# An encoder trunk on one core: first transfers in the order of need, the second chunk of x turned later, inverse square roots by three Newton steps

## The chip, the cores and the metric

The kernel runs on one core of one Trainium2 chip. The metric is device time of one launch in microseconds. TensorE is called PE, VectorE DVE, ScalarE ACT, GpSimd POOL; SP is the engine that only issues transfers. ACT and POOL issue transfers too, each in its own queue.

## The reference

Two layers over 512 tokens of 1024 features, all in float32. Each layer normalises x, projects it by one combined matrix, runs two attentions (a windowed one with 8 query and 2 key heads, and one over a two-dimensional neighbourhood with 8 heads), mixes them by sigmoid gates, and adds a SwiGLU block. The start of the first layer is what matters here:

```python
def rms_norm(x, g):
    xf = x.astype(jnp.float32)
    y = xf * lax.rsqrt(jnp.mean(xf * xf, axis=-1, keepdims=True) + EPS)
    return (y * g.astype(jnp.float32)).astype(x.dtype)
...
    for l in range(DEPTH):
        h = rms_norm(x, attn_norm_g[l])
        z = jnp.einsum('bsd,dc->bsc', h, w_in[l])
        qa, ka, va, qb, kb, vb, ga, gb = jnp.split(z, IN_SPLITS, axis=-1)
        qa = apply_rope(rms_norm(qa.reshape(b, s, A_HEADS, HEAD_DIM), q_norm_a[l]), cos, sin)
        ka = apply_rope(rms_norm(ka.reshape(b, s, A_KV_HEADS, HEAD_DIM), k_norm_a[l]), cos, sin)
```

Every normalisation is an inverse square root, of the whole row or of each head's 64 features.

## The kernel before, in words

Every float32 operand is split in a high part and a low part, and a product is three matmuls: high by high, high by low, low by high. Activations lie transposed, features on the partitions: x is eight chunks of 128 features by 512 tokens. The scaling by the row's inverse square root is applied after the products, so they need not wait for it.

**The start.** x comes in eight transfers of 256 KB on SP's queue (`x_load`, line 720), in pieces of 512 bytes. The weights of the first projection (queries, 512 columns) come as four slabs of 512 KB, two chunks each (`first_load`, line 536): the first on ACT's queue in two halves, the others on POOL's. PE warms up with seven products of a zero tile (`turn_over`, line 707). `token_matmul` (line 905) then takes the chunks: `begin(k)` is `start` (line 1209), which turns chunk k by four matmuls with an identity, has ACT make the high part of chunk k, a copy and its squares, and DVE the low part, the sum of squares and the weights' low part (`first_parts`, line 548; the weights' high part is a cast by ACT, by DVE for chunk 0). For a chunk, twelve products follow in three groups of four (one for each block of 128 tokens): high x by high weight, high x by low weight, low x by high weight. Behind a chunk's first group stands the turn of the chunk two further on:

```python
            begin(0)
            begin(1)
            tick(0.0)
```

so chunks 0 and 1 are turned ahead of the first product.

**Inverse square roots.** `rsqrt` (line 832) starts from an integer shift of the bits and refines by four Newton steps of three DVE instructions each. It is called twelve times: for each layer twice for the rows' norm (4 columns) and four times for the heads' (`head_scale`: 32 columns three times, 8 columns once).

**What sets the order.** The program is written by Python in one pass that keeps a clock for each engine. The main stream of products yields after each unit; attention heads, tables and norms are chains that are let in (`issue`, line 394) where the clocks say their operands are ready. Weight slabs are issued by the position of PE's stream (`tick`). The pass runs once dry, to learn when each buffer lives, then buffers are packed into two arenas, and the pass runs again and replays the choices. So a change of the first instructions or of a cost moves later choices too. Whether ACT or DVE scales a block of probabilities is such a choice. A transfer's completion is counted on one of eight semaphores of its kind in turn; a transfer that takes one again waits for the one that had it.

Of the kernel before, what the change touches and what calls it, by code (L numbers as in the profile page):

```python
# [12 lines left out]
F32 = mybir.dt.float32  # L13
# [3 lines left out]
ALU = mybir.AluOpType  # L17
AX = mybir.AxisListType

P = 128  # L20
# [5 lines left out]
KD = D // P  # L26
# [183 lines left out]
def trunk(ctx: ExitStack, tc: tile.TileContext, a: dict, out: bass.AP, lay: Layout):  # L210
    nc = tc.nc
    PS = bass.MemoryType.PSUM
    cp = ctx.enter_context(tc.tile_pool(name="cp", bufs=1))
# [7 lines left out]
    def nm(s):  # L221
        uid[0] += 1
        return f"{s}_{uid[0]}"
# [7 lines left out]
    def buf(shape, dtype=F32):  # L231

        n = int(np.prod(shape))
        x = lay.place(n, dtype)
        t = arenas[dtype][:, x : x + n]
        if len(shape) == 2:
            t = t.rearrange("p (a b) -> p a b", b=shape[1])
        elif len(shape) == 3:
            t = t.rearrange("p (a b c) -> p a b c", b=shape[1], c=shape[2])
        return t  # L240
# [7 lines left out]
    def mm_bank():  # L248
        return pm.tile([P, S], F32, tag="mm", name=nm("mm"))
# [4 lines left out]
    def small(w, dtype=F32):  # L254
        return sp.tile([P, w], dtype, tag=f"s{w}_{dtype}", name=nm("sm"), bufs=6)
# [81 lines left out]
    V = Engine(nc.vector, "dve")  # L337
    A = Engine(nc.scalar, "act")
    G = Engine(nc.gpsimd, "pool")
    Q = Engine(nc.sync, "dma")  # L340
    AQ = Engine(nc.scalar, "dma")
# [95 lines left out]
    def tick(dt):  # L437
        pos[0] += dt
        while due and due[0][0] <= pos[0]:
            due.pop(0)[2]()  # L440
# [79 lines left out]
    highs, lows, raws, used = {}, {}, {}, [0]  # L520
# [12 lines left out]

    FIRST = KD // 2

    def first_load(i):

        n1, n2, ((_, ap),) = plan[i]
        raws[i] = buf([n1, n2])
        ap = ap.rearrange("(k p) n -> p k n", p=P)  # L540
        if i:
            GQ.dma_start(raws[i], ap)
        else:
            for k in range(2):
                AQ.dma_start(raws[i][:, k], ap[:, k])
        highs[i], lows[i] = buf([n1, n2], F32R), buf([n1, n2], F32R)

    def first_parts(k):
# [25 lines left out]
    def w_take():  # L574

        i = used[0]
        used[0] += 1
        w_load(i)
        w_low(i)
        return [(highs[i][:, k], lows[i][:, k]) for k in range(plan[i][0])]  # L580
# [108 lines left out]
    def mm(ps, l_, r_, start, stop):  # L689
        T.matmul(ps, l_, r_, start=start, stop=stop, skip_group_check=True)  # L690
# [11 lines left out]
    ones = cp.tile([P, 2], F32, tag="ones", name="ones")  # L702
# [4 lines left out]
    def turn_over(n):  # L707

        ps = mm_bank()
        for _ in range(n):  # L710
            T.matmul(ps[:, :P], idle, idle, start=True, stop=True)
# [8 lines left out]
    def x_load(c):  # L720
        t = act().rearrange("p (b n) -> p b n", b=NB)
        Q.dma_start(t, xv[:, :, P * c : P * c + P])
        xin.append(t)
# [3 lines left out]
    Q.dma_start(ident, a["consts"][:, :P])  # L727
    rows_of = lambda n: a[n].rearrange("l (k p) -> (l k) p", p=P)
    AQ.dma_start(vec, rows_of("attn_norm_g"))
    first_load(0)  # L730
    AQ.dma_start(vec2[16:32], rows_of("ffn_norm_g"))
    for c in range(KD):
        x_load(c)
    first_load(1)
    posi = cp.tile([P, P], I32, tag="posi", name="posi")
    for h in range(2):
        GQ.dma_start(
# [3 lines left out]
    def gains_b(i, n):  # L741
        for h in range(2):
            GQ.dma_start(vec2[2 * i : 2 * i + 2, HD * h : HD * h + HD], a[n])

    gains_b(0, "q_norm_b")
    gains_b(1, "k_norm_b")
    first_load(2)
    first_load(3)
    gqa = cp.tile([P, 2, DEPTH, HD], F32, tag="gqa", name="gqa")
# [2 lines left out]
    snk = cp.tile([P, DEPTH, 8], F32, tag="snk", name="snk")  # L752
    GQ.dma_start(snk, a["sink_a"].rearrange("l h -> (l h)").unsqueeze(0).to_broadcast([P, DEPTH * 8]))
    GQ.dma_start(cst[:, P:], a["consts"][:, P:])
    warm = cp.tile([P, 2], F32, tag="warm", name="warm")
    A.copy(warm, ones)
    turn_over(7)
    ps = at_bank()
    T.transpose(ps[:, :16], vec, ident[:16, :16])
# [71 lines left out]

    def rsqrt(dst, src, w):

        ki, y, t = small(32, I32), small(32), small(32)
        V.tensor_scalar(ki[:, :w], src.bitcast(I32), 1, None, ALU.logical_shift_right)
        V.tensor_tensor(y[:, :w].bitcast(I32), magic[:, :w], ki[:, :w], ALU.subtract)
        for it in range(4):
            V.tensor_tensor(t[:, :w], y[:, :w], y[:, :w], ALU.mult)
            V.scalar_tensor_tensor(t[:, :w], t[:, :w], -0.5, src, ALU.mult, ALU.mult)
            V.scalar_tensor_tensor(dst if it == 3 else y[:, :w], t[:, :w], 1.5, y[:, :w], ALU.add, ALU.mult)  # L840

    class Norm:

# [17 lines left out]
        def chain(self):  # L861

            yield Need(keys=[f"acc{self.i}"])
            yield Need("pe", [self.acc], [at_slots])
            at_slots.take()
            ps = at_bank()
            for b in range(NB):
                T.matmul(ps[:, b : b + 1], self.acc[:, P * b : P * b + P], ones[:, 0:1], start=True, stop=True)
            ms = small(32)
            V.tensor_scalar(ms[:, :NB], ps[:, :NB], 1.0 / D, EPS, ALU.mult, ALU.add)  # L870
            at_slots.give(clock["dve"])
            self.rst = cp.tile([P, NB], F32, tag="rstd", name=nm("rstd"), bufs=2)
            rsqrt(self.rst, ms[:, :NB], NB)
            done.add(f"rst{self.i}")
            yield Need("pe", [self.rst], [at_slots])
            at_slots.take()
            ps = at_bank()
            for b in range(NB):
                T.transpose(ps[:, P * b : P * b + P], self.rst[:, b : b + 1].to_broadcast([P, P]), ident)
            self.rows = buf([S])  # L880
            V.tensor_copy(self.rows, ps)
            at_slots.give(clock["dve"])
            done.add(f"rows{self.i}")
# [21 lines left out]
    def token_matmul(nrm, evac, begin=None):  # L905

        ps = [mm_bank() for _ in range(NB)]
        if begin is not None:
            begin(0)
            begin(1)  # L910
            tick(0.0)
        for k0 in range(0, KD, 2):
            wk = w_take()
            order = [(b, k) for b in range(NB) for k in range(2)]
            if begin is not None:
                order.sort(key=lambda x: x[1])
                if k0 + 2 < KD:
                    for k in range(2):
                        kk = k0 + k
                        for part in range(3):  # L920
                            for b in range(NB):
                                x = (nrm.xl if part == 2 else nrm.xh)[kk][:, P * b : P * b + P]
                                mm(ps[b], x, wk[k][part == 1], kk == part == 0, False)
                            if not part and kk + 2 < KD:
                                begin(kk + 2)
                            tick(NB * UNIT / 3)
                            yield UNIT
                    continue
            for i, (b, k) in enumerate(order):
                t = slice(P * b, P * b + P)  # L930
                kk = k0 + k
                hi, lo = wk[k]
                mm(ps[b], nrm.xh[kk][:, t], hi, kk == 0, False)
                mm(ps[b], nrm.xh[kk][:, t], lo, False, False)
                mm(ps[b], nrm.xl[kk][:, t], hi, False, kk == KD - 1)
                tick(UNIT)
                if kk == KD - 1:
                    evac(b, ps[b])
                yield UNIT
# [5 lines left out]
    def head_scale(raw, nh, rst, res):  # L945

        ss = small(32)
        for b in range(NB):
            yield Need("act", [raw[b]])
            sq = act()  # L950
            A.activation(sq[:, : nh * HD], raw[b], AF.Square)
            yield Need("dve", [sq])
            V.tensor_reduce(ss[:, b * nh : b * nh + nh], per_head(sq[:, : nh * HD]), AX.X, ALU.add)
        yield Need()
        w = NB * nh
        rb = rst.unsqueeze(2).to_broadcast([P, NB, nh])
        v = lambda t: t[:, :w].rearrange("p (b h) -> p b h", h=nh)
        t = small(32)
        V.tensor_tensor(v(t), v(ss), rb, ALU.mult)
        V.tensor_tensor(v(t), v(t), rb, ALU.mult)  # L960
        V.tensor_scalar(t[:, :w], t[:, :w], 1.0 / HD, EPS, ALU.mult, ALU.add)
        f = sp.tile([P, 32], F32, tag="hf", name=nm("hf"), bufs=4)
        rsqrt(f[:, :w], t[:, :w], w)
        V.tensor_tensor(v(f), v(f), rb, ALU.mult)
        res.append(f)
# [263 lines left out]
    def layer(l):  # L1229
# [173 lines left out]
        spawn(chain_parts())  # L1403

        yield from token_matmul(nrm, copy_to(qraw), (lambda *x: start(nrm, *x)) if l == 0 else None)
        done.add(f"q{l}")

# [8 lines left out]
        for i, unit in enumerate(pair_matmul(KD, nrm.xh, nrm.xl, kv_evac)):  # L1416
            yield unit
            if i == KD:
                yield f"rows{nrm.i}"
        done.add(f"kv{l}")  # L1420
        yield from token_matmul(nrm, copy_to(qk[0]))
        done.add(f"qk{l}0")

# [370 lines left out]
```

## Time and profile before

| what | us |
|---|---|
| three timed runs | 1381.34 (median), 1382.67, 1380.99 |
| the profiled execution, its own time | 1382.42 |
| its span on the core | 1380.6 |
| PE busy | 1371.4 (99%) |
| weight loads of PE (beside its matmuls) | 1215.7 (88%) |
| DVE, ACT, POOL busy | 909.6, 708.8, 316.2 |

The span runs from the first to the last instruction on the core; the execution's own time has 1.8 us around it. Weight loads run beside matmuls and are counted apart. [...]

### The profile page before, as it was taken

To read this page: it belongs to the slowest core of one execution; us is meant where nothing else is said; L and a number is where in the kernel's file an instruction comes from. 1 tells how busy PE (TensorE), PEld (TensorE's weight loads), DVE (VectorE), ACT (ScalarE), POOL (GpSimd) and SP (SyncE) were. 2 spreads that over 40 slices of the span, in tenths; PEclk is the share of its full clock that TensorE was granted. 3 is DMA by queue.
4 is the path that set the end of the run, shared out by engine and by line. 5 is a ranking of instruction groups with operands and counts; after the bars stand their busy time and mean duration, and the time that the engine had idled before them with its cause. 6 is when DMAs were issued, how large, how long until landed. Compare 5 with 4: busy or idle time off the path is not lost.

```text
span 1380.6 us, 20976 instructions
## 1 busy us (share of the span) xinstructions
PE 1371.4 (99%) x8074; PEld 1215.7 (88%) x8074; DVE 909.6 (66%) x1700; ACT 708.8 (51%) x1174; POOL 316.2 (23%) x327
## 2 busy tenths in 40 slices
PE   8999999999999999999999999999999999999998
PEld 7888888888899999999888888888889999999997
DVE  5876878455966657575648668784568747575653
ACT  6477667534744333343545675684456434333441
POOL 4542222310311110111353422222012110111111
PEclk9999999999999999999999999999999999999999
DMA  8997888973766484734899978879439483655536
GB/s 215 180 176 136 165 154 155 180 190 104 151 152 153 111 195 91 183 93 92 170 192 191 167 136 156 165 138 233 120 93 214 104 214 93 153 121 124 132 67 153
DMA packets 192357, 207.48 MB, mean 150 GB/s; under 512 B 25584, under 2 KB 159136, under 8 KB 192256
## 3 DMA queue, kind: packets, MB, share of 16 engines
q0 software_dynamic: 132928, 141.54, 54.9%
q1 hardware_dynamic: 58832, 63.91, 16.1%
q8 instruction: 64, 1.05, 0.3%
q10 hardware_dynamic: 496, 0.67, 0.2%
q14 instruction: 37, 0.30, 0.1%
HBM read 193.51 MB, written 2.10 MB: 142 GB/s over the span
## 4 chain that ended last, share of the span: by engine, by line
PE 94%; DVE 2%; issue 1%; DMA 1%; POOL 1%; ACT 1%; SPq 0%; POOLq 0%; ACTq 0%; DVEq 0%
PE mm L310 72%; PE at L310 21%; DVE arena L310 1%; POOL arena L310 1%; DVE sm L310 1%; DMA arena<-in_w_in 1%; DMA arena<-in_x 1%; ACT arena L310 1%; ACT L310 0%; SPq L310 0%; DVE hf L310 0%; ACT trig L310 0%; ACT sm L310 0%; DVE den L310 0%; POOLq L310 0%
## 5 line engine op out<-in xcount | busy, mean ns | idle before, releaser
L310 PE MATMUL mm<-arena 128*128 128x512 f32 (+1 forms) x5568 | 1109.0, 355 | 0.2
L310 PEld LDWEIGHTS mm<-arena 128*128 128x128 f32 x5568 | 904.2, 190 | 131.4 <-issue 0.6
L310 ACT CAST arena<-arena 128x1024 fp32r<-128x1024 f32 (+2 forms) x277 | 234.6, 871 | 212.3 <-DVE arena L310 205.2
L310 DVE TENSOR_TENSOR arena<-arena,arena 128x1024 fp32r<-128x1024 f32 (+2 forms) x268 | 262.0, 993 | 48.3 <-ACT arena L310 44.3
L310 PE MATMUL at<-arena 128*128 128x256 f32 (+1 forms) x1964 | 285.0, 289 | 0.3 <-DVE negm L310 0.2
L310 ACT ACTIVATE arena<-arena 128x1024 fp32r<-128x1024 f32 (+3 forms) x252 | 207.0, 843 | 150.1 <-DMA arena<-in_w_down 63.9
L310 PEld LDWEIGHTS at<-arena 128*128 128x128 f32 x1964 | 261.7, 191 | 14.1 <-DVE negm L310 1.2
L310 DVE TENSOR_TENSOR arena<-arena,mm 128x512 f32<-128x512 f32 x144 | 98.7, 685 | 242.3 <-PE mm L310 240.7
L310 POOL DMA_DIRECT2D arena<-in_w_in x163 | 161.8, 1367 | 307.2 <-ACT arena L310 289.4
L310 POOL DMA_DIRECT2D arena<-in_w_down x96 | 99.2, 1230 | 508.9 <-ACT arena L310 310.6
L310 DVE TENSOR_TENSOR arena<-arena 128x1024 f32<-128x1024 f32 (+3 forms) x196 | 158.1, 823 | 2.3
L310 DVE TENSOR_TENSOR arena<-at,arena 128x512 fp32r<-128x512 f32 (+4 forms) x158 | 104.2, 660 | 31.6 <-ACT arena L310 22.6
L310 ACT CAST arena<-at 128x512 fp32r<-128x512 f32 (+2 forms) x116 | 64.3, 554 | 62.6 <-PE at L310 61.2
L310 ACT ACTIVATE arena<-arena,negm 128x256 f32<-128x256 f32 (+1 forms) x128 | 68.2, 533 | 18.7 <-DVE negm L310 16.9
L310 PE MATMUL at<-cst,arena 128*128 128x128 f32 x472 | 72.6, 276 | 4.0 <-DMA arena<-in_x 3.8
L310 PEld LDWEIGHTS at<-cst,arena 128*128 128x128 f32 x472 | 57.7, 141 | 13.4 <-DMA arena<-in_x 4.1
L310 DVE TENSOR_TENSOR arena<-mm,arena 128x512 f32<-128x512 f32 x72 | 49.1, 687 | 22.7 <-PE mm L310 22.3
L310 ACT COPY arena<-at 128x512 f32<-128x512 f32 (+1 forms) x72 | 41.3, 585 | 43.5 <-PE at L310 42.9
L310 DVE CUSTOM_DVE_ANT_0 arena<-at,cst,nsnk 128x256 f32<-128x256 f32 (+1 forms) x64 | 34.4, 548 | 33.4 <-PE at L310 32.6
L310 DVE CUSTOM_DVE_ANT_0 arena<-at,arena 128x256 f32<-128x256 f32 x64 | 26.4, 420 | 20.9 <-PE at L310 20.6
L310 POOL DMA_DIRECT2D arena<-in_w_up x8 | 8.2, 1028 | 122.4 <-PE mm L310 67.9
L310 ACT ACTIVATE arena<-arena,vec2T 128x512 fp32r<-128x512 f32 x16 | 11.6, 726 | 47.6 <-DVE arena L310 47.6
(75 smaller groups left out, 434.5 us busy)
## 6 DMA issues: line engine op xcount, KB each, us to landing
arena<-in_w_in POOLq DMA_DIRECT2D x99, 512.0 KB, 7.3
arena<-in_w_down POOLq DMA_DIRECT2D x80, 512.0 KB, 6.8
arena<-in_w_gate SPq DMA_DIRECT2D x20, 1024.0 KB
arena<-in_w_up SPq DMA_DIRECT2D x20, 1024.0 KB
arena<-in_w_in POOLq DMA_DIRECT2D x64, 256.0 KB, 6.6
arena<-in_w_proj_a POOLq DMA_DIRECT2D x16, 512.0 KB, 7.6
arena<-in_w_proj_b POOLq DMA_DIRECT2D x16, 512.0 KB, 7.0
arena<-in_w_out SPq DMA_DIRECT2D x16, 512.0 KB
```

Of the source, the lines that this page charges most:

```text
L310: f(*args, **kw)
```

## The change

The first weight slab's second half is issued behind ACT's table load and a small copy that triggers it. The second slab is issued behind the two loads of positions on POOL's queue. Chunk 1 is turned behind chunk 0's first group of products and chunk 2 behind its second; from chunk 3 on nothing moves. `rsqrt` makes three steps in place of four.

```diff
--- before.py
+++ after.py
@@ -533,7 +533,7 @@
 
     FIRST = KD // 2
 
-    def first_load(i):
+    def first_load(i, between=None):
 
         n1, n2, ((_, ap),) = plan[i]
         raws[i] = buf([n1, n2])
@@ -541,8 +541,9 @@
         if i:
             GQ.dma_start(raws[i], ap)
         else:
-            for k in range(2):
-                AQ.dma_start(raws[i][:, k], ap[:, k])
+            AQ.dma_start(raws[i][:, 0], ap[:, 0])
+            between()
+            AQ.dma_start(raws[i][:, 1], ap[:, 1])
         highs[i], lows[i] = buf([n1, n2], F32R), buf([n1, n2], F32R)
 
     def first_parts(k):
@@ -727,11 +728,11 @@
     Q.dma_start(ident, a["consts"][:, :P])
     rows_of = lambda n: a[n].rearrange("l (k p) -> (l k) p", p=P)
     AQ.dma_start(vec, rows_of("attn_norm_g"))
-    first_load(0)
+    warm = cp.tile([P, 2], F32, tag="warm", name="warm")
+    first_load(0, lambda: A.copy(warm, ones))
     AQ.dma_start(vec2[16:32], rows_of("ffn_norm_g"))
     for c in range(KD):
         x_load(c)
-    first_load(1)
     posi = cp.tile([P, P], I32, tag="posi", name="posi")
     for h in range(2):
         GQ.dma_start(
@@ -742,6 +743,7 @@
         for h in range(2):
             GQ.dma_start(vec2[2 * i : 2 * i + 2, HD * h : HD * h + HD], a[n])
 
+    first_load(1)
     gains_b(0, "q_norm_b")
     gains_b(1, "k_norm_b")
     first_load(2)
@@ -752,8 +754,6 @@
     snk = cp.tile([P, DEPTH, 8], F32, tag="snk", name="snk")
     GQ.dma_start(snk, a["sink_a"].rearrange("l h -> (l h)").unsqueeze(0).to_broadcast([P, DEPTH * 8]))
     GQ.dma_start(cst[:, P:], a["consts"][:, P:])
-    warm = cp.tile([P, 2], F32, tag="warm", name="warm")
-    A.copy(warm, ones)
     turn_over(7)
     ps = at_bank()
     T.transpose(ps[:, :16], vec, ident[:16, :16])
@@ -831,13 +831,14 @@
 
     def rsqrt(dst, src, w):
 
+
         ki, y, t = small(32, I32), small(32), small(32)
         V.tensor_scalar(ki[:, :w], src.bitcast(I32), 1, None, ALU.logical_shift_right)
         V.tensor_tensor(y[:, :w].bitcast(I32), magic[:, :w], ki[:, :w], ALU.subtract)
-        for it in range(4):
+        for it in range(3):
             V.tensor_tensor(t[:, :w], y[:, :w], y[:, :w], ALU.mult)
             V.scalar_tensor_tensor(t[:, :w], t[:, :w], -0.5, src, ALU.mult, ALU.mult)
-            V.scalar_tensor_tensor(dst if it == 3 else y[:, :w], t[:, :w], 1.5, y[:, :w], ALU.add, ALU.mult)
+            V.scalar_tensor_tensor(dst if it == 2 else y[:, :w], t[:, :w], 1.5, y[:, :w], ALU.add, ALU.mult)
 
     class Norm:
 
@@ -907,7 +908,6 @@
         ps = [mm_bank() for _ in range(NB)]
         if begin is not None:
             begin(0)
-            begin(1)
             tick(0.0)
         for k0 in range(0, KD, 2):
             wk = w_take()
@@ -921,7 +921,9 @@
                             for b in range(NB):
                                 x = (nrm.xl if part == 2 else nrm.xh)[kk][:, P * b : P * b + P]
                                 mm(ps[b], x, wk[k][part == 1], kk == part == 0, False)
-                            if not part and kk + 2 < KD:
+                            if not kk and part < 2:
+                                begin(1 + part)
+                            elif not part and kk + 2 < KD:
                                 begin(kk + 2)
                             tick(NB * UNIT / 3)
                             yield UNIT
```

On PE, at its start: `at` tiles are chunks being turned (the first `at` is chunk 0), the `mm` tile fed from `trig` is the zero product, the four other `mm` tiles are the four token blocks of the projection. Before:

```order
L310 MATMUL at_134<-cst,arena_72 128x128 x4
L310 MATMUL mm_139<-trig 128x128 x3
L310 MATMUL at_149<-cst,arena_72 128x128 x4
L310 MATMUL mm_130<-arena_73 128x512
L310 MATMUL mm_131<-arena_73 128x512
L310 MATMUL mm_132<-arena_73 128x512
L310 MATMUL mm_133<-arena_73 128x512
L310 MATMUL at_166<-cst,arena_72 128x128 x4
L310 MATMUL mm_130<-arena_73 128x512
```

With the change:

```order
L310 MATMUL at_134<-cst,arena_72 128x128 x4
L310 MATMUL mm_139<-trig 128x128 x3
L310 MATMUL mm_130<-arena_73 128x512
L310 MATMUL mm_131<-arena_73 128x512
L310 MATMUL mm_132<-arena_73 128x512
L310 MATMUL mm_133<-arena_73 128x512
L310 MATMUL at_154<-cst,arena_72 128x128 x4
L310 MATMUL mm_130<-arena_73 128x512
L310 MATMUL mm_131<-arena_73 128x512
L310 MATMUL mm_132<-arena_73 128x512
L310 MATMUL mm_133<-arena_73 128x512
L310 MATMUL at_170<-cst,arena_72 128x128 x4
```

The turn of chunk 1 has moved from ahead of the first group to behind it, and the turn of chunk 2 from behind the first group to behind the second.

On ACT, its first transfers, with what they wait for: `vec` and `vec_76` take gains, `arena_72` here the weight halves. Before:

```order
L310 DMA vec<-in_attn_norm_g 16x128
L310 DMA arena_72<-in_w_in 128x512 x2
L310 DMA vec_76<-in_ffn_norm_g 16x128 [waits Pool_49]
L310 ACT_TABLE_LOAD
L310 COPY warm<-ones 128x2 [waits Pool_49]
L310 ACTIVATE arena_73<-at_134,vecT 128x512 [waits DVE_49,PE_49]
```

With the change:

```order
L310 DMA vec<-in_attn_norm_g 16x128
L310 DMA arena_72<-in_w_in 128x512
L310 ACT_TABLE_LOAD
L310 COPY warm<-ones 128x2 [waits Pool_49]
L310 DMA arena_72<-in_w_in 128x512
L310 DMA vec_76<-in_ffn_norm_g 16x128 [waits DMAHW0_49]
L310 ACTIVATE arena_73<-at_134,vecT 128x512 [waits DVE_49,PE_49]
```

The second half has moved behind the table load and the copy, and the second load of gains with it.

On POOL, its first transfers, the large ones being the weight slabs of chunks 2 and 3, 4 and 5, 6 and 7; `DMASW0` is the semaphore that the queue's first transfer took. Before:

```order
L310 DMA arena_72<-in_w_in 128x2x512
L310 DMA posi<-in_positions 4x8x8 x2
L310 DMA vec_76<-in_q_norm_b 2x64 [waits Pool_49]
L310 DMA vec_76<-in_q_norm_b 2x64
L310 DMA vec_76<-in_k_norm_b 2x64 x2
L310 DMA arena_72<-in_w_in 128x2x512
L310 DMA arena_72<-in_w_in 128x2x512 [waits DMASW0_49]
```

With the change:

```order
L310 DMA posi<-in_positions 4x8x8 x2
L310 DMA arena_72<-in_w_in 128x2x512
L310 DMA vec_76<-in_q_norm_b 2x64 [waits Pool_49]
L310 DMA vec_76<-in_q_norm_b 2x64
L310 DMA vec_76<-in_k_norm_b 2x64 x2
L310 DMA arena_72<-in_w_in 128x2x512
L310 DMA arena_72<-in_w_in 128x2x512 [waits DMASW0_49]
```

The positions have moved ahead of the first slab of this queue; the last of the three slabs waits for `DMASW0` in both, which was the first slab's and is now the positions'.

PE has the same 8050 matmuls in both. DVE loses the 36 of the Newton steps, and eight scalings of probabilities that were ACT's are DVE's in the new plan.

## Rows read from the trace of the kernel before

**Rows 1.** The page: the span, and busy time of each engine.

```profile
span 1380.6 us, 20976 instructions
...
PE 1371.4 (99%) x8074; PEld 1215.7 (88%) x8074; DVE 909.6 (66%) x1700; ACT 708.8 (51%) x1174; POOL 316.2 (23%) x327
```

**Rows 2.** What PE's matmuls waited for: us in total, times, longest.

```profile
PE at L310 <- DMA arena<-in_x: 3.8, 2, 2.3
...
PE at L310 <- DVE negm L310: 0.2, 1, 0.2
```

**Rows 3.** Timeline of PE: start, length, instructions merged, idle time before them.

```profile
1.00 3.36 PE L310 MATMUL mm<-trig 128*128 128x128 f32 x14 [1.00 <-POOL trig L310]
...
6.05 0.66 PE L310 MATMUL at<-cst,arena 128*128 128x128 f32 x4 [1.48 <-DMA arena<-in_x]
...
6.55 0.83 PE L310 MATMUL mm<-trig 128*128 128x128 f32 x6
...
9.69 1.11 PE L310 MATMUL at<-cst,arena 128*128 128x128 f32 x4 [2.31 <-DMA arena<-in_x]
...
10.46 2.05 PE L310 MATMUL mm<-arena 128*128 128x512 f32 x4
...
19.82 0.60 PE L310 MATMUL at<-cst,arena 128*128 128x128 f32 x4
```

**Rows 4.** The chain that ended last, up to 40 us: start, length, what.

```profile
1.65 7.99 DMA arena<-in_x
...
17.23 2.76 PE mm L310 x12
19.98 0.44 PE at L310 x4
```

**Rows 5.** Windows: busy time of each engine, then PEclk, DMA share, GB/s.

```profile
7.00:8.00 1.00, 0.38 (x4) 0.19 (x2) 0.06 (x1) 0.97 (x3) 0.00 (x0) 0.93 1.10 308
8.00:9.00 1.00, 0.00 (x0) 0.00 (x0) 0.69 (x1) 1.00 (x2) 0.00 (x0) 0.50 1.20 265
14.00:15.00 1.00, 1.00 (x4) 0.83 (x3) 0.40 (x1) 0.97 (x3) 0.48 (x1) 0.66 1.06 337
20.00:25.00 5.00, 5.00 (x28) 4.12 (x27) 3.68 (x12) 3.49 (x7) 0.00 (x0) 1.00 0.71 139
```

**Rows 6.** Timeline of ACT: table load, chunk 0's high part, chunk 1's weight cast.

```profile
2.75 1.28 ACT L310 ACT_TABLE_LOAD   x1 [2.75 <-issue]
...
6.75 0.69 ACT L310 ACTIVATE arena<-at,vecT 128x512 fp32r<-128x512 f32 x1 [2.51 <-PE at L310]
...
8.48 0.60 ACT L310 CAST arena<-arena 128x512 fp32r<-128x512 f32 x1
```

**Rows 7.** Queues (q0 POOL, q10 ACT, q1 SP), 5-7.5, then 14.5-18 us.

```profile
q0 software_dynamic: 150, 0.50, 51.9%
q10 hardware_dynamic: 162, 0.25, 28.8%
q1 hardware_dynamic: 391, 0.20, 27.3%
...
q0 software_dynamic: 481, 1.07, 98.7%
q1 hardware_dynamic: 185, 0.09, 9.8%
```

**Rows 8.** Timeline of POOL: the first transfers that it issues.

```profile
1.38 0.86 POOL L310 DMA_DIRECT2D arena<-in_w_in  x1 [0.20 <-issue]
...
2.23 1.25 POOL L310 DMA_DIRECT2D posi<-in_positions  x2
...
9.38 0.73 POOL L310 DMA_DIRECT2D arena<-in_w_in  x1 [3.11 <-DMA arena<-in_w_in]
```

**Rows 9.** DVE's small tiles: one group of lines; then the scalings, min/median/max ns.

```profile
L310 DVE SCALAR_TENSOR_TENSOR sm<-sm,sm 128x32 f32<-128x32 f32 x42 | 8.1, 192 | 1.4
...
L310 DVE TENSOR_SCALAR arena<-arena,sm x88: 341/354/799, 81.5 to 927.9; 128x256 f32<-128x256 f32 x61, 128x384 f32<-128x384 f32 x27
```

## The prediction

> **What bounds the kernel now.** First the span and the engines' busy times: TensorE (PE) is busy for 1371.4 of 1380.6 us, and no other engine is above 66% [rows 1]. So the end moves only if PE starts useful work sooner or stands less. Next, what PE waited for: 3.8 us on two transfers of x, and 0.2 us on a softmax maximum from VectorE (DVE) [rows 2]. What can be won is therefore in the first 20 us; all behind it is one packed stream of matmuls that moves as a block.
>
> [...] PE turns chunk 0 of x, multiplies zeros (six records up to 7.38 us), then stands 2.31 us for chunk 1 of x, though chunk 0 could be multiplied already: its first product starts at 10.46, behind chunk 1's turn [rows 3]. The chain that ended last says the same: 7.99 us of it are a transfer of x, which ends at 9.64 [rows 4]. [...]
>
> **The change part by part.** *Order on PE.* Chunk 0's first four products now stand ahead of chunk 1's turn, and chunk 2's turn ahead of chunk 0's last four. Common point: the turn of chunk 4, at 19.82 us [rows 3]. Ahead of it, counted from chunk 0's first product, stand in both orders 28 products (three times twelve less the eight of chunk 2 that follow) and the turns of chunks 1 to 3. At full clock twelve products take 2.76 us on the chain and a turn 0.44 [rows 4], so 28 x 0.23 + 3 x 0.44 = 7.76 us. (Before, one turn of the three already stood ahead of the first product.) The first product needs the high part of chunk 0, which ScalarE (ACT) ends at 6.75 + 0.69 = 7.44 [rows 6]. With no wait and full clock chunk 4's turn starts at 15.2: **4.6 us sooner**, the upper end.
>
> Two things take from this. The first is chunk 1's landing. The four products end at about 8.4; if chunk 1 still lands at 9.64, PE restarts at 9.69 with 24 products and three turns left, 6.84 us, and reaches the point at 16.5: 3.3 us sooner. The second is the clock. [...] How long it stays down I take from what PE did before the clock rose, twice in this trace: at the very start it had worked 3.36 us without a break (14 records, 0.24 us each; the six behind the next turn took 0.14 each) [rows 3], and before 14.7 it had worked 5.0 us. A slow stretch of 3.4 us from 7.9 costs 1.7, one as long as before (6.8 us) costs 3.4. Taken together: no slow stretch 4.6 (3.3 with chunk 1 late); a short one 2.9 (2.5 with chunk 1 late); the long one 1.2 (0.8). **I take 2.9**, because PE now works through from 7.44 and the steady start is the nearest row; the ends 0.8 and 4.6 stay for the range.
>
> *Transfers.* Does chunk 1 land sooner? From 5 to 7.5 us x got 0.20 MB, while the second weight slab on POOL's queue got 0.50 and the first on ACT's 0.25 [rows 7]. The slab is now issued behind the two position loads, 1.25 us later [rows 8], so chunk 1 has that much more of the engines to itself. I count it as landed when the four products end, at 8.4 to 8.8. [...]
>
> *ACT's queue.* The second half of the first weight slab now stands behind the table load, 1.28 us, and a tiny copy, so some 1.5 us later. Its cast began at 8.48 [rows 6], straight behind ACT's own work; 1.5 us later it ends at 10.6. The products that read it come at 7.44 + 12 x 0.23 + 2 x 0.44 = 11.1 at the earliest. Cost nothing; the cover is chunk 0's twelve products, and without it the price is 1.5 us. SP's queue holds x alone; its fourth load no longer waits for the gains, its last now waits for chunk 1 instead of the weight half, and both have landed when their turn comes.
>
> *POOL's queue.* The fourth weight slab waits for the queue's first transfer. That was the second slab, and POOL stood 3.11 us for it, up to 9.38 [rows 8]; now it is the positions, so this load may go out up to 3.1 us sooner and meet chunks 4 to 7. Chunk 4's turn found its data at 19.82; now it is wanted at 15.2 to 17. I count nothing, and price it as the rival on the other side.
>
> *Newton steps.* Twelve inverse square roots lose three instructions each: 36 on DVE, at 0.192 us or less [rows 9], under 6.9 us. Eight scalings of probabilities move from ACT to DVE in the new plan (88 to 96 there, 0.354 us each, 2.8 us). All of it lies beside PE: the list of its waits knows none on these tiles, and 0.2 us on DVE in all [rows 2]. Credit 0, bound 0.2; without that cover a root on the path would be worth its three instructions, 0.6 us.
>
> Sum: 2.9 us off. The profiled execution took 1382.42 us, its span 1380.6 and 1.8 around it; less 2.9 is 1379.5. It lies 1.08 above the median of the three timed runs (1381.34), which differ by 1.7 us among themselves. [...] I read half of the 1.08 as a start that came out worse than usual, and **forecast 1382.4 - 0.5 - 2.9 = 1379.0 us**.
>
> **The rivals.** *No slow stretch (0.18).* [...] Then 4.6 off, 1382.4 - 0.5 - 4.6 = 1377.3.
>
> *The slab meets chunks 2 and 3, or the clock stays low as long as before (0.20).* Half a megabyte, at the 0.95 MB that all queues moved in those 2.5 us [rows 7], holds up x for 1.3 us; chunk 2 is wanted at about 10, not at 12.3. Gain 0.8 to 1.6: 1382.4 - 0.5 - 1.6 = 1380.3, to 1381.1.
>
> *Nothing kept (0.05).* The shift is taken back by weights that land no sooner, as those of the next stage at 40 us. Against it: the transfer engines are busy for only 0.71 of the stretch from 20 to 25 us [rows 5], so later loads, which are issued as PE and ACT go, can shift with them. 1381.5.
>
> *Slower (0.05): POOL's loads starve chunk 4.* From 14.5 to 18 us POOL's queue took 1.07 MB and x 0.09 [rows 7]. If the early fourth slab lets POOL's loads run through ahead of chunk 4, it lands when they end, at about 23 (the 0.71 busy share from 20 to 25), and PE stands from 15.2 until then: 23 - 19.8 = 3.2 us later than before, 1385.1. It makes the kernel slower from a landing after 19.8, and by more than 0.2% from 22.6. Against it: before, chunk 4 was there at 19.82 without a wait, with the same loads in the queues, and it stands in SP's queue ahead of that slab.
>
> **How the numbers follow.** 0.2% of 1381.34 is 2.8 us, about what a measurement of this kernel can tell from no change; the line is at 1378.6. The forecast case (gain 2 to 3.7 us, 1378.1 to 1380) has 0.50, of which 0.22 lies below that line; with the 0.18 and 0.02 for help from the shorter DVE chains, **faster 0.42**. The rest of it, 0.28, with 0.20 and 0.05 is **same 0.53**; **slower 0.05**. The range goes from the full 4.6 (1376.9, with the median's scatter) to nothing kept (1381.6).
>
> **What would show it.** In the new profile: PE's first products at about 7.5; the wait on x down from 3.8 to 1.5 to 2.5 us; chunk 4's turn at 16 to 17.5; granted clock low from about 8 to 11.5; DVE some 4 us less busy; PE's waits behind 20 us still under 2 us together. Wrong would be: a wait on x of over 1 us at chunks 2 to 4, a slow clock up to 14, or a stage behind 40 us in which PE newly stands.

## The result and the profile after

The changed kernel takes 1385.80 us (median of 8 runs, 1383.95 to 1389.94); the kernel before takes 1381.48 on the same chip (8 runs, 1380.64 to 1382.67). The ratio is 1.0036 with a 95% interval of 1.0026 to 1.0045: slower by some 4 to 5 us, where 2.3 us off the earlier median had been forecast. The profiled execution took 1385.41 us. Its page, to be held against [rows 1]:

```profile
span 1383.6 us, 20943 instructions
...
PE 1372.9 (99%) x8074; PEld 1215.8 (88%) x8074; DVE 905.3 (65%) x1672; ACT 704.3 (51%) x1166; POOL 318.6 (23%) x327
```

DVE is 4.3 us less busy, ACT 4.5 us less, and the span is 3.0 us longer all the same. **The start did what was wanted, and more.** PE's timeline (start, length, what, idle time before), to be held against [rows 3]:

```profile
5.47 1.12 PE L310 MATMUL at<-cst,arena 128*128 128x128 f32 x4 [0.90 <-DMA arena<-in_x]
6.38 1.49 PE L310 MATMUL mm<-trig 128*128 128x128 f32 x6
7.52 1.71 PE L310 MATMUL mm<-arena 128*128 128x512 f32 x4
9.08 0.60 PE L310 MATMUL at<-cst,arena 128*128 128x128 f32 x4
...
15.94 0.60 PE L310 MATMUL at<-cst,arena 128*128 128x128 f32 x4
```

The first products start at 7.52 us, not 10.46; chunk 1 is turned at 9.08 without a wait; the turn of chunk 4 is at 15.94 instead of 19.82, 3.9 us sooner. PEclk is the clock granted to PE as a share of full clock. The windows (PE busy, PEclk, DMA share, GB/s) that had 0.93, 0.50 and 0.66 in [rows 5] now read 1.00:

```profile
7.00:8.00 1.00, 1.00 (x6) 1.00 1.20 305
8.00:9.00 1.00, 1.00 (x4) 1.00 1.05 363
14.00:15.00 1.00, 1.00 (x6) 1.00 1.10 323
```

The first two of these are not the full clock. PEclk reads 1.00 also where the trace holds no record of the clock, and here the first record, of full clock, begins at 8.71 us. What PE did until then is seen in the lengths of its instructions: chunk 0's turn takes 1.12 us, like chunk 1's at 9.69 under a clock of 0.50 before, where 0.60 is the length at full clock, and the six zero products take 1.49 us, where they took 0.83 before [rows 3, rows 5]. So PE works at about half speed, the lower level, up to about 8.7 us and at full clock from there on: the turn at 9.08 takes 0.60. What is gone is the fall at 7.9 us, with the slow work up to 14.7 behind it: the trace of the kernel before has records of 0.50 from 7.86 to 14.69 us.

The queues from 5 to 7.5 us (packets, MB, share of the engines' time), to be held against [rows 7], show x (q1) with 0.51 MB, 0.20 before, and POOL's queue (q0) with next to nothing:

```profile
q1 hardware_dynamic: 1022, 0.51, 80.2%
...
q0 software_dynamic: 73, 0.04, 7.2%
```

In POOL's timeline the last of its three slabs goes out at 7.07 us, 9.38 before [rows 8], and harms nothing:

```profile
7.07 0.73 POOL L310 DMA_DIRECT2D arena<-in_w_in  x1 [0.39 <-DMA posi<-in_positions]
```

**The loss is where nothing was edited.** What PE waited for (us in total, times, longest), to be held against [rows 2]:

```profile
PE mm L310 <- DMA arena<-in_w_down: 3.6, 2, 1.9
...
PE at L310 <- DVE arena L310: 1.0, 3, 0.4
PE at L310 <- DMA arena<-in_x: 0.9, 1, 0.9
```

The wait on x is down from 3.8 to 0.9 us. A wait of 3.6 us on `w_down` is new. PE's timeline has it once in each layer, ahead of the first `w_down` products of the feed-forward block:

```profile
388.10 4.28 PE L310 MATMUL mm<-arena 128*128 128x512 f32 x29 [1.75 <-DMA arena<-in_w_down]
...
1069.87 6.29 PE L310 MATMUL mm<-arena 128*128 128x512 f32 x31 [1.88 <-DMA arena<-in_w_down]
```

Behind the second one the clock fell as well (windows, as above):

```profile
1068.00:1070.00 2.00, 0.13 (x1) 1.00 1.29 252
1070.00:1071.00 1.00, 1.00 (x3) 0.63 0.27 42
1071.00:1073.00 2.00, 2.00 (x10) 0.50 0.02 3
1073.00:1075.00 2.00, 2.00 (x16) 0.83 0.00 0
```

From 1070 to 1075 that is 0.37 + 1.0 + 0.34 = 1.7 us of work lost to the lower clock (the trace has it at 0.50 from 1070.25 to 1073.67), where the kernel before has 1.00 in each of these windows. Standing and clock together are 3.6 + 1.7 = 5.3 us; less the 3.9 of the start it makes +1.4 of the +3.0. Of the remaining 1.6 us, 1.1 are small waits behind the start that were not there before, on DVE above all (1.0 us in the list above); what the other 0.5 are is not shown.

**Why `w_down` was late.** These weights come as a high part (a transfer on POOL's queue) and a low part (ACT writes the negated high part, then a transfer on POOL's queue adds the original to it). SP's queue brings `w_gate` and `w_up` in slabs of two halves, 1 MB each. SP's timeline (start, length, what) of the kernel before, then of the one after:

```profile
350.63 24.85 SPq L310 DMA_DIRECT2D arena<-in_w_up  x2
387.29 11.29 SPq L310 DMA_DIRECT2D arena<-in_w_gate  x2
```

```profile
336.55 36.65 SPq L310 DMA_DIRECT2D arena<-in_w_up  x2
376.18 20.93 SPq L310 DMA_DIRECT2D arena<-in_w_gate  x2
```

The first half of the next `w_gate` slab went out at 387.29 before, and goes out at 376.18 now. The transfers on `w_down` issued from 350 to 392 us (the last line of the view of this tensor), before and after:

```profile
DMA to landing us min/median/max: 4.7/7.9/9.6
```

```profile
DMA to landing us min/median/max: 6.2/10.8/13.8
```

They take up to 13.8 us, not 9.6. The slowest of them is the one that PE waits for: the chain that ended last, after the change, has it end at 388.06 us, where PE's products start at 388.10.

```profile
374.25 13.81 DMA arena<-in_w_down
```

The queues tell why. From 373 to 386 us after:

```profile
q0 software_dynamic: 1282, 1.26, 60.7%
q1 hardware_dynamic: 1055, 2.10, 51.2%
```

and from 376 to 388 us before:

```profile
q0 software_dynamic: 1686, 1.65, 76.8%
q1 hardware_dynamic: 528, 1.05, 30.8%
```

SP's queue (q1) moves two halves of slabs where it moved one, and POOL's queue (q0) gets less. Nothing in the diff says so. But the Python pass that writes the program runs dry first, on clocks charged for every instruction, and packs the buffers by what it learns there. Twelve roots that are charged three DVE instructions less give another packing, and a slab on SP's queue starts when the last reader of its new place is done; this is read from the program, not from a trace. The dry run itself is blind to this: it has a transfer start no sooner than 3 us ahead of PE's clock (`start = max(start, clock["pe"] - 3.0)`), while SP issues it as soon as its place is free.

### The profile page after: what moved, and what is told of

Its sections match the earlier page's. It is cut to its first block, busy times and chain, and to the rows that moved or that the text cites. A ratio compares the mean times of both kernels' runs of the same rounds, so it can differ in the third digit from the quotient of the medians.

```text
span 1383.6 us, 20943 instructions
## 1 busy us (share of the span) xinstructions
PE 1372.9 (99%) x8074; PEld 1215.8 (88%) x8074; DVE 905.3 (65%) x1672; ACT 704.3 (51%) x1166; POOL 318.6 (23%) x327
## 3 DMA queue, kind: packets, MB, share of 16 engines
q8 instruction: 64, 1.05, 0.3%
## 4 chain that ended last, share of the span: by engine, by line
PE 90%; DMA 3%; issue 2%; DVE 2%; ACT 2%; POOL 1%; SPq 0%; POOLq 0%
PE mm L310 71%; PE at L310 20%; DMA arena<-in_w_down 2%; ACT arena L310 1%; DVE arena L310 1%; DVE sm L310 1%; POOL arena L310 1%; DMA arena<-arena 1%; DMA arena<-in_x 0%; ACT L310 0%; DVE hf L310 0%; ACT sm L310 0%; SPq L310 0%; DVE den L310 0%; DVE rstd L310 0%
## 5 line engine op out<-in xcount | busy, mean ns | idle before, releaser
L310 DVE TENSOR_TENSOR arena<-arena 128x1024 f32<-128x1024 f32 (+4 forms) x196 | 158.2, 824 | 2.3
```

The costliest lines, as they stand in the source:

```text
L310: f(*args, **kw)
```

## The experiments

All twelve kernels were timed in five rounds beside the kernel before (1381.46 to 1381.69 us in the three groups). "Ratio" is against it, with a 95% interval. Theory A, that the new plan makes the loss, has two forms from the second group on: A1 that the `w_gate` slab shares the engines with the `w_down` transfers, A2 that POOL's own order is to blame.

### Which part of the change loses: four kernels

`start_only` is the changed kernel with four Newton steps, `newton_only` the kernel before with three:

```diff
-        for it in range(3):
+        for it in range(4):
```

> The new start with four Newton steps. Theory A (the plan): the planner's dry run charges VectorE for each instruction; with three steps it packs the arena's buffers and orders the FFN's transfers in another way, and in that plan SyncE's 1 MB slab of w_gate starts 11 us sooner (376.18 us after, 387.29 before), beside the POOL transfers that bring the low parts of w_down, which then land late. Four steps give back the old plan behind the start, so only the start's gain is left: 1381.5 - 3.9 = 1377.6 us (1376.8 to 1378.4), and no wait of PE on w_down over 1 us. Theory B (the cover was used up): the low part of w_down landed at nearly the same moment in both kernels (387.76 before, 388.06 after) while PE came 3 us sooner; then the sooner start alone brings the wait, and the time is 1381 to 1386 us with PE standing 1 to 2 us on w_down in each layer.

> The old start with three Newton steps. Theory A (the plan): the whole loss without the start's gain, 1385.8 + 3.9 = 1389.7 us (1387 to 1391), with PE standing about 2 us on w_down at the first FFN products of each layer. Theory B (the cover was used up by the sooner start): as before, 1381.5 us (1380.5 to 1382), and no wait on w_down.

`three_planned_as_four` executes three steps and charges the dry run with four; `four_planned_as_three` the reverse:

```diff
-        for it in range(3):
+        steps_here = 4 if lay.dry else 3
+        for it in range(steps_here):
```

> The whole change, but the dry run, which sets buffers and order, is charged with four Newton steps while three are executed. Theory A (the plan): 1377.6 us (1376.8 to 1378.4), within 0.3 us of the kernel with the new start and four steps, and no wait of PE on w_down over 1 us. Theory B (the sooner start uses up the cover): 1381 to 1386 us. Theory C (three steps executed do the harm themselves, by VectorE running ahead and taking buffers or queue places sooner): about 1385.8 us.

> The new start; four Newton steps executed, while the dry run is charged with three. Theory A (the plan): the loss stays, 1385.8 us (1384 to 1388), with the two waits on w_down of about 2 us. Theory C (three steps executed do the harm themselves): 1377.6 us without those waits.

| kernel | steps run | steps planned | us | ratio | wait on `w_down`, us |
|---|---|---|---|---|---|
| start_only | 4 | 4 | 1378.71 | 0.9979 (0.9971 to 0.9988) | none |
| three_planned_as_four | 3 | 4 | 1378.59 | 0.9977 (0.9969 to 0.9986) | none |
| four_planned_as_three | 4 | 3 | 1389.81 | 1.0063 (1.0051 to 1.0076) | 4.6 |
| newton_only (old start) | 3 | 3 | 1390.04 | 1.0064 (1.0050 to 1.0077) | 5.3 |

The plan decides, not the steps: with the plan for four the wait is gone and the start's gain is left, whether three steps run or four. Theories B and C fall. Both kernels with that plan lie 0.2 to 0.3 us above the range expected of them, which took the 3.9 us of one trace for the gain. PE's waits of `start_only`, then of `newton_only`:

```profile
PE at L310 <- DMA arena<-in_x: 1.6, 1, 1.6
PE mm L310 <- POOL trig L310: 1.0, 1, 1.0
PE at L310 <- DVE negm L310: 0.2, 1, 0.2
```

```profile
PE mm L310 <- DMA arena<-in_w_down: 5.3, 2, 3.2
PE at L310 <- DMA arena<-in_x: 2.2, 2, 1.2
```

`four_planned_as_three` missed its range by 2 us upwards: besides `w_down` PE stood 2.2 us on DVE, where the changed kernel has 1.0. I read this as a plan that has not counted the fourth step and is later still when it is there; no run took it apart.

### What in the plan loses: the slab held, and the slab added

`held_slab` keeps the changed kernel and its plan, and holds back both halves of one `w_gate` slab per layer:

```diff
                 t = buf([4, 512])
+                if self.col == 768 and self.later and not lay.dry:
+                    A.copy(t[:, 0, 0:2], ones)
```

> The whole change and its own plan, except that the two halves of each layer's second w_gate slab (column 768, 1 MB each on SyncE's queue) are held back to their place in the program by a two-element ScalarE copy into each half's buffer; in the trace after, the first half started at 376.18 us, beside the POOL transfers that the first w_down products wait for. Theory A1 (shared transfers): without the slab beside them these POOL transfers land in about 9 us instead of 13 to 14, PE stands under 0.5 us on w_down, and the time falls by the two waits (3.6 us) and part of the lower clock behind the second one: 1380.0 to 1382.5 us. Rival A2 (order on POOL's own queue): the w_down transfers are late since POOL issues the first quad's low parts ahead of them; then the slab is beside the point, the waits stay at about 2 us each and the time at 1385.8 us (1384.5 to 1388).

It takes 1380.50 us, ratio 0.9989 (0.9980 to 0.9997): 5.3 us less than the changed kernel by the medians (6.5 by the two ratios), about the 5.3 that standing and clock had cost in its trace. SP's timeline has the slab at its place in the program, and the `w_down` transfers issued from 350 to 392 us land sooner:

```profile
399.91 1.74 SPq L310 DMA_DIRECT2D arena<-in_w_gate  x2
```

```profile
DMA to landing us min/median/max: 4.1/6.2/10.4
```

PE's matmuls wait for `w_down` no more. So A1 holds in this direction, with POOL's order left as it was, and without the hold SP ran 399.91 - 376.18 = 23.7 us ahead of the place where the program, and the planner with it, has this transfer. The other direction adds the rival to the plan that loses nothing. `twin_slab` has the good plan of `start_only` and one extra megabyte per layer; `twin_two` has two:

```diff
             self.raw = []
+            if self.col == 768 and self.later and not lay.dry:
+                Q.dma_start(out[0, :, :512], self.w[:512, 768:1280])
```

> The new start with four Newton steps, whose plan loses nothing, plus in each layer one extra transfer of 1 MB on SyncE's queue (a block of w_gate copied into rows of the output that are written anew at the end), issued right behind the second w_up slab, which is where the other plan starts its w_gate slab. Theory A1 (shared transfers): the POOL transfers of w_down take about 13 us instead of 9, which uses up the margin of 2.0 us that they had in the kernel without the extra transfer; PE stands 1 to 2.5 us on w_down in each layer and the time is 1381 to 1385 us. Rival A2 (POOL's own order): 1378.7 us, no wait on w_down.

> As the kernel with one extra 1 MB transfer per layer, but with two of them, 2 MB per layer, in the same place. With one the four POOL transfers took 11.7 to 12.3 us, PE stood 0.2 to 0.6 us on w_down and the time rose by 1.0 us. Theory A1 (shared transfers): a dose that doubles, so 13 to 15 us for these transfers, PE standing 1.5 to 3 us in each layer, 1382 to 1385 us. Rival (only one slab of a queue is ever moved beside them, so a second one adds nothing): 1379.7 us.

`twin_slab` takes 1379.67 us (ratio 0.9988, 0.9979 to 0.9997), `twin_two` 1392.83 (1.0075, 1.0062 to 1.0088). The waits of PE and the landing of the `w_down` transfers (350 to 392 us) of `twin_slab`, then of `twin_two`:

```profile
PE mm L310 <- DMA arena<-in_w_down: 0.8, 2, 0.6
```

```profile
DMA to landing us min/median/max: 4.2/8.4/12.3
```

```profile
PE mm L310 <- DMA arena<-in_w_down: 8.6, 2, 4.5
```

```profile
DMA to landing us min/median/max: 6.4/13.8/17.7
```

Both expectations were missed on the size, low for one and high for two, and both fall to A1 in kind: the slowest landing goes from 9.6 us (`start_only`) to 12.3 and 17.7. The first megabyte delays the landing by 2.7 us and PE by 0.6, so some 2 us of margin pay for most of it; the second meets PE in full (8.6 us in two waits) and then the clock, which `twin_two` has at half behind both waits. The extra transfer writes to DRAM, not to on-chip memory, so its price need not be that of a slab.

### Where the start's gain comes from: three kernels

`turns_only` is the kernel before with the two `begin` hunks of the diff alone; `transfers_only` has the hunks of `first_load`, `warm` and the POOL order alone; `pool_order_only` only the move of the second slab. All have four Newton steps and the plan for four.

> The kernel before with only PE's order changed: chunk 1 of x turned behind chunk 0's first four products; four Newton steps, transfers as before. As the prediction has it, the start's gain comes from this order alone (first products fill the wait for chunk 1, and no slow clock follows a stand of 2 us): 1378.7 us (1378.2 to 1379.7). Rival (the transfers carry it): 1380.8 to 1381.8 us.

> The kernel before with only the transfers and the table load in the new order (positions ahead of the second w_in slab on POOL, the table load between the first slab's halves on ScalarE); PE's order and four Newton steps as before. As the prediction has it (these moves cost and bring nothing while chunk 1 is turned before any product): 1381.5 us (1380.8 to 1382). Rival (they carry the gain): 1378.7 to 1379.7 us.

> The kernel before with one move: the second w_in slab goes onto POOL's queue behind positions and the small gains; ScalarE's queue, the table load, PE's order and the four Newton steps as before. Both the turns alone and the transfers alone brought the whole start gain, so the step 'the moved transfers cost and bring nothing' fell. Theory T1 (the second slab's packets take room from chunk 1 of x): in the first 7 us POOL's queue moved 0.39 MB before and nothing with the new transfers, while x on SyncE's queue went from 0.53 to 0.79 MB; this move alone then gives 1379.0 us (1378.4 to 1379.8). Rival T2 (the table load 1.1 us earlier on ScalarE carries it): 1381.5 us (1380.8 to 1382).

They take 1378.77 (0.9979, 0.9970 to 0.9987), 1378.99 (0.9982, 0.9974 to 0.9991) and 1378.62 us (0.9979, 0.9970 to 0.9988). Each part alone brings the whole gain, and both together bring no more (1378.71). `transfers_only` missed what was expected of it: 1381.5 us, no gain, by the prediction's own reasoning. PE's timeline of `turns_only`, then of `pool_order_only`:

```profile
6.84 1.20 PE L310 MATMUL mm<-arena 128*128 128x512 f32 x4
8.96 0.66 PE L310 MATMUL at<-cst,arena 128*128 128x128 f32 x4 [0.92 <-DMA arena<-in_x]
```

```profile
7.89 1.06 PE L310 MATMUL at<-cst,arena 128*128 128x128 f32 x4
8.61 1.43 PE L310 MATMUL mm<-arena 128*128 128x512 f32 x4
9.87 0.60 PE L310 MATMUL at<-cst,arena 128*128 128x128 f32 x4
```

In the first, chunk 1 still comes late (8.96, before 9.69), but work lies ahead of it: PE stands 0.92 us. In the second, chunk 1 has landed when it is wanted at 7.89. Neither shows the fall of [rows 5]. By the lengths the first is at full clock in these lines already (0.66 us for a turn), and the second is at the lower level until about 9 us: 1.06 us for the turn at 7.89, 0.60 for that at 9.87. What moves chunk 1 is seen in the queues from 0 to 7 us, of the kernel before and of `pool_order_only`:

```profile
q1 hardware_dynamic: 1066, 0.53, 26.3%
q0 software_dynamic: 99, 0.39, 14.4%
```

```profile
q1 hardware_dynamic: 1656, 0.82, 41.9%
...
q0 software_dynamic: 54, 0.00, 0.6%
```

x (q1) gets 0.82 MB where it got 0.53, since the slab's 0.39 MB are out of its way. T1 holds; the table load is not needed for it.

### Two more plans

The changed kernel executing three steps, its dry run charged with two, then with five (`steps_here = 2 if lay.dry else 3`, and 5). Which instruction the slab waits for was read from the programs beforehand.

> The whole change, three Newton steps executed, the dry run charged with two: a third plan. In it the first half of the second w_gate slab waits in the first layer for a late ScalarE activation (as late as in the kernel before), in the second layer for an early VectorE subtraction (the same place as in the kernel after). Theory A1 (what counts is when this slab is let go beside the w_down transfers): no wait on w_down over 1 us in the first layer's FFN, one of 1.5 to 2.5 us in the second's; 1380 to 1384 us. Rival A3 (any plan made for fewer VectorE instructions is too tight everywhere): two waits of about 2 us, 1385 us or more.

> The whole change, three Newton steps executed, the dry run charged with five: a fourth plan. In it the slab's first half waits for a late ScalarE activation in both layers. Theory A1: no wait on w_down over 1 us in either layer, 1378 to 1380.5 us. Rival (plans other than the one the kernel was brought up with lose at this place): waits of about 2 us in both layers, 1383 us or more.

`planned_as_two` takes 1385.89 us (1.0030, 1.0018 to 1.0042), `planned_as_five` 1384.40 (1.0022, 1.0014 to 1.0031). PE's waits of the first, and of the second:

```profile
PE mm L310 <- DMA arena<-in_w_down: 2.6, 1, 2.6
PE at L310 <- DVE arena L310: 1.8, 2, 1.5
```

```profile
PE at L310 <- DVE arena L310: 4.2, 4, 1.4
```

On `w_down` both are as A1 said: one wait, in the second layer (ahead of 1069.73 us; 2.6 us, where at most 2.5 had been expected), where the slab goes out at 1056.93, and none in the plan that lets it go at 1068.91. On the time both missed, since each plan brings new waits elsewhere, on DVE. So of the plans for two, three, four and five steps, with the new start and three steps run, the one for four is the best by 5.8 us or more (1385.89, 1385.80, 1378.59, 1384.40): the charge picks a plan, and a smaller charge does not pick a better one. `three_planned_as_four` beats both kernels, by 2.9 and 7.2 us.

## Why the prediction was wrong

- **The step that failed** is in its first paragraph: "all behind it is one packed stream of matmuls that moves as a block". Up to the first feed-forward block the stream did move, by some 3 us (its first 24 products of 128 by 256 start at 374.20 us, before at 377.37), but it was no longer the same stream. The front of this text says that a change of a cost moves later choices; the prediction carried that only as far as eight scalings that go from ACT to DVE. It did not ask where buffers land, and so when SP's slabs are let go. Price: 7.1 us by the medians (1385.80 against 1378.71 of `start_only`). Of these `held_slab` gives back 5.3. Its trace still has 1.0 us of waits on DVE and 0.9 on a transfer between buffers, where `start_only` has 0.2 in all behind the start; that is about the other 1.8, though no run took these waits away.
- **The start's gain** came out at the size forecast: 2.9 us forecast, 2.9 (0.21%) by the ratio of `start_only`. That is in part luck, since the clock did something else than the sum has it do. The 3.9 of the trace are one execution, with chunk 0 turned at 5.47 us and chunk 4 at 15.94; `start_only`, `three_planned_as_four` and `four_planned_as_three` have this at 5.32 to 6.17, and chunk 4's turn at 16.57 to 16.77 us.
- **The clock** in the start was foreseen wrong. The forecast was a slow stretch of 3.4 us from 7.9 us on, at a cost of 1.7. No run whose start is shown has such a stretch: the kernel before has 6.83 us at 0.50, and the changed kernel has the lower level from the start to 8.71 us and no fall until 1070.25 us; chunk 0's products, from 7.52 on, lost some 0.6 us to it (half of 1.19). In place of the 1.7 us put down for a slow stretch, that gives 15.2 + 0.6 = 15.8 for chunk 4's turn, and it was at 15.94. The rival "no slow stretch" did not happen either. The products began at 7.52, just as said, and the wait on x was 0.9, not 1.5 to 2.5.
- **The slow stretch of the kernel before** is not in each of its runs. Of the 76 runs listed with a clock beside the twelve kernels, 19 have the 0.997 of the profiled one, with a median of 1381.92 us, and 43 have 1.000, with 1381.36 (time without a record of the clock counts as 1). So the 0.5 us that the prediction took off for a start worse than usual, an estimate of its author's, is about what the record has. The one other profile with the old start, `newton_only`, has no fall in the start, by the lengths: PE is at the lower level in the turns at 5.58, 9.15 and 11.77 us (1.12, 1.12, 1.06) and at full clock in that at 15.73 (0.60), and chunk 4 is turned at 18.94, not 19.82.
- **Where the gain comes from** was half right. The prediction gave it to PE's order and treated POOL's move as what that order needs to find chunk 1 in time. Each is enough alone: chunk 0's products fill part of the stand of 2.31 us [rows 3], or chunk 1 comes in time, and in either trace PE does its first products sooner (at 6.84 and 8.61 us, not 10.46) and, by the lengths, at full clock from about 9 us or before. The prediction counted POOL's slab as 1.25 us later; in the first 7 us of `pool_order_only` none of its 0.39 MB is left beside x.
- **ACT's queue and the fourth slab** cost nothing, as said. The rival on the slower side (chunk 4 starved, 1385.1 us) has nearly the time that came out, and is not what happened: chunk 4 is turned at 15.94 without a wait, a little ahead of the forecast of 16 to 17.5.
- **Newton steps**: credit 0, as said, for the instructions: 1378.71 with four and 1378.59 with three, in one plan. DVE is 4.3 us less busy, foreseen as some 4. The bound, 0.2 us, was one for the instructions and left the plan out.
- **What would show it wrong** was named: "a stage behind 40 us in which PE newly stands". It is there, twice, and PE's waits behind 20 us come to 4.9 us, not to under 2.

## What to carry to other kernels

Where a program is planned from a cost model, an edit is two changes: what it executes, and the plan that its cost picks; charging the plan with the old cost separates them in one run, and here kept the gain. A transfer without a clock of its own in the plan starts when its buffer comes free (here 23.7 us ahead of its place), so after a re-plan look at when each large transfer is let go and which small ones, with what margin, run beside it. Here two cures of the same wait did not add up. And where a column of the profile says full clock at the very start, hold the lengths of the instructions against it (here 1.12 us for a turn that takes 0.60 at full clock).

## What the runs showed of the hardware

**Transfers beside each other.** With 2.10 MB beside it instead of 1.05, POOL's queue had its `w_down` transfers land after up to 13.8 us instead of 9.6. In the 13 us from 373 the two queues moved 1282 and 1055 packets, and SP's, with twice the bytes in each, 63% of the bytes; how the queues are served no run shows.

**The clock behind a stand.** Stands of PE of nearly one length went either way. The granted clock was still 1.00 after 1.75 us (first layer of the changed kernel), 2.10 (second layer of `newton_only`) and 2.12 us (first layer of `four_planned_as_three`); it fell after 1.88 (second layer of the changed kernel), 2.51 and 2.62 (second layer of `four_planned_as_three` and of `planned_as_two`) and 3.21 (first layer of `newton_only`). The second layer of `newton_only`, then its first (windows: PE busy, PEclk, DMA share, GB/s):

```profile
1076.00:1078.00 2.00, 1.89 (x12) 1.00 0.18 29
```

```profile
392.00:394.00 2.00, 1.44 (x3) 0.56 0.24 43
394.00:396.00 2.00, 2.00 (x11) 0.58 0.00 1
```

So the stand of 2.10 us cost its 2.10 us, and that of 1.88 us cost, with the clock, 3.6 (1.88 + 1.7); one trace can't tell which is usual. The changed kernel's runs differ by 6.0 us among themselves, and those of the kernel before by 2.0. I read part of this as such stands going one way in one run and the other way in the next, which was not shown. The clocks on record point that way and no further: the changed kernel's two fastest runs (1383.95 and 1384.09) have 1.000 and its slowest (1389.94) 0.998, but 1389.20 has 0.999, like 1385.41.

**The clock at the start.** The first clock record, of full clock, begins at 4.45 us in the trace of the kernel before and at 8.71 in that of the changed one. Up to chunk 4's turn, PE does the same work in the same order in the kernel before and in `newton_only`; yet the turn of chunk 0 and the six zero products take 0.66 and 0.83 us in the first, 1.12 and 1.49 in the second. In four profiles with the whole new start they take 1.11 to 1.12 and 1.49, and the first turn of 0.60 us starts at 9.08 us (changed kernel), 9.73 (`start_only`), 11.08 (`four_planned_as_three`) and 11.29 (`three_planned_as_four`). I read this as a level that differs from one execution to the next, by which one trace can't judge a start.
